# A PEER layer's look-ups: the factor of the gathered rows in PSUM, a quarter of the low parts on VectorE, and another order of choices

## The chip, the cores and the metric

The kernel runs on one core of a Trainium2 chip. The metric is the device time of one execution in microseconds (us). The engines are PE (TensorE), DVE (VectorE), ACT (ScalarE), POOL (GpSimd) and SP (SyncE, here only a queue that starts DMAs).

## The reference, cut to what matters

The program is two transformer blocks on 512 tokens of width 1024. Only the last layer of the second block changes, a mixture of 16384 tiny experts (128 x 128 keys), of which each token uses 8 x 16:

```
q = (xt @ w_q).reshape(T, H, 2, PEER_DKEY // 2)
s = jnp.einsum('thcd,hcnd->thcn', q, sub_keys).astype(jnp.float32)
top_s, top_i = lax.top_k(s, K)
cand = (top_s[:, :, 0, :, None] + top_s[:, :, 1, None, :]).reshape(T, H, K * K)
...
best_s, best_j = lax.top_k(cand, K)
expert = jnp.take_along_axis(cand_i, best_j, axis=-1)
g = jax.nn.softmax(best_s, axis=-1).astype(u.dtype)
...
act = jax.nn.gelu(jnp.einsum('cd,chkd->chk', xc, u_tab[ec]), approximate=False)
return jnp.einsum('chk,chkd->cd', gc * act, v_tab[ec])
```

## The kernel before, in words

The tokens lie in four groups of 128. For group 0 and half of group 1 (64 tokens) the rows of `u_tab` that were chosen are gathered from HBM by indirect DMAs, 128 rows of 4 KB to a fetch, and multiplied by the token (`gscr`, on DVE, which sums as it multiplies). For the remaining 320 tokens the product with all 16384 rows of `u` is computed densely, in 128 blocks (`expert_block`): a block loads 512 KB of `u` (`wraw`, by SP), ACT rounds it to a high part `whi`, POOL subtracts to get the low part `wlo`, and PE makes 24 matmuls of 320 columns from the parts. Three buffers hold `wraw`, three `whi` and `wlo`.

`route` makes queries, scores and the two stages of top-k (`choose`, on DVE), and writes out where each chosen expert stands as a dense table `Gd` (`gates`: one-hot tables `oh` by DVE, scaled by ACT, multiplied on PE into `pg`, copied by ACT to `stg`, written by SP). Beside it run the dense blocks, whose results go to HBM (`Ad`). `combine` then reads `v_tab` (`vraw`), `Gd` (`rgat`) and `Ad` (`ract`) and adds up the result in PSUM: 128 times 18 matmuls of 512 columns (`acc`). What blocks and fetches `route` did not get to is done there.

The order is set by code: `route` goes block by block, adds `UCOST` to a credit, and emits pieces of the routing work (`choose` and `gates` are generators whose `yield` gives a cost) while the credit is positive. After each block it issues up to `RATE` steps of `gathered`; a step is one fetch (on POOL's queue) and the product of the row fetched six steps before. `self.limit` holds the steps back until the indices are known. There are 332 steps (192 fetches of `u` rows, 128 of `v` rows, and two lags of 6). `combine` spreads what steps are left evenly over its units, one for each of the 128 additions and one for each block still to be made. Engines work in order, each through its own list.

Of the kernel before, what the change touches and what calls it, by code (L numbers as in the profile page):

```python
# [7 lines left out]
F32 = mybir.dt.float32  # L8
# [4 lines left out]
AF = mybir.ActivationFunctionType  # L13
# [24 lines left out]
LEAD = 2  # L38
FLEAD = 4
LAST = 3  # L40
GCOST = 0.4
UCOST = 1.7
AHEAD = 3
RATE = 1.5


class Stream:


    def __init__(self, nc, pool, chunks, raw_bufs, split_bufs):  # L50
        self.nc, self.pool, self.chunks = nc, pool, chunks
        self.raw_bufs, self.split_bufs = raw_bufs, split_bufs
        self.raw, self.parts = {}, {}
        self.nd = self.ns = self.ng = 0
        self.on_vector, self.all_vector = ("cw1",), False

    def _load(self):
        i = self.nd
# [6 lines left out]
    def _split(self):  # L65
        i = self.ns
        while self.nd <= i:
            self._load()
        w = self.chunks[i][2]
        raw = self.raw.pop(i)  # L70
        hi = self.pool.tile([P, 1024], F32R, name=f"whi{i}", tag="whi", bufs=self.split_bufs)
        lo = self.pool.tile([P, 1024], F32R, name=f"wlo{i}", tag="wlo", bufs=self.split_bufs)
        self.nc.scalar.activation(hi[:, :w], raw[:, :w], AF.Copy)  # L73
        if self.all_vector or self.chunks[i][0] in self.on_vector and i % 2:
            self.nc.vector.tensor_tensor(lo[:, :w], raw[:, :w], hi[:, :w].bitcast(F32), op=ALU.subtract)
        else:
            self.last_split = self.nc.gpsimd.tensor_tensor(lo[:, :w], raw[:, :w], hi[:, :w].bitcast(F32),  # L77
                                                           op=ALU.subtract)
        self.parts[i] = (hi, lo)
        self.ns += 1  # L80
# [18 lines left out]
class Kernel:  # L99
# [1141 lines left out]
    def gathered(self, ep):  # L1241
# [11 lines left out]
        def after():  # L1253
            return self.tc.issue_after(self.last_gate.ins) if self.last_gate else ExitStack()

        jobs = [(self.xidx, k, self.xx, self.xact) for k in range(NX)]
        jobs += [(self.gidx, k, self.xr, self.gact) for k in range(P)]
        rows = {}
        for k in range(self.nu + lag):
            if k < self.nu:  # L1260
                rows[k] = fetch(a["peer_ur_2"], *jobs[k][:2])
            if k >= lag:
                _, c, x, acc = jobs[k - lag]
                scr = ep.tile([P, D], BF16, name="gscr", tag="gscr", bufs=1)
                with after():
                    nc.vector.scalar_tensor_tensor(scr, rows.pop(k - lag), 1.0, x, op0=ALU.mult,  # L1266
                                                   op1=ALU.mult, accum_out=acc[:, c:c + 1])
            if k == self.nu + lag - 1:
                self.act(self.gact, self.gact, AF.Gelu)
                nc.vector.tensor_tensor(self.gw, self.gw, self.gact, op=ALU.mult)  # L1270
            yield
# [22 lines left out]
    def route(self, ep, rp, pp):  # L1294
        tc, nc, a = self.tc, self.nc, self.a
        sk = rp.tile([P, 16, P], F32, name="sk", tag="cand")
        nc.sync.dma_start(sk, a["peer_sk"])

        iota_s = rp.tile([P, P], F32, name="iota", tag="tables")
# [30 lines left out]
            return qt  # L1330

        def scores(b, q):
            pc = pp.tile([P, 4, P], F32, name="psc", tag="psc", bufs=4)
            for tb in range(4):
                nc.tensor.matmul(pc[:, tb, :], q[:, tb * P:(tb + 1) * P], sk[:, b, :], start=True, stop=True)
            for tb in range(4):
                topk(tv[:, tb, b], tix[:, tb, b], pc[:, tb, :], mr[:, :P])
# [133 lines left out]
        def gates(tb, p0=0, p1=4):  # L1471
# [6 lines left out]
            for part in range(p0, p1):  # L1478
                self.write(len(self.pieces) - P // PIECE)
                stg = self.cp.tile([P, P, 32], F32, name="stg", tag="xlo" if part % 2 else "xhi")  # L1480
                for k in range(8):
# [1 line left out]
                    if x + 4 * AHEAD < 32 * p1:  # L1483
                        oh[x + 4 * AHEAD] = onehots(t, x + 4 * AHEAD)
                    J, I = oh.pop(x)
                    pg = pp.tile([P, 4, P], F32, name="pg", tag="psc", bufs=4)
                    for c in range(4):
                        nc.tensor.matmul(pg[:, c, :], J[:, c], I[:, c], start=True, stop=True)  # L1488
                    nc.scalar.activation(stg[:, :, 4 * k:4 * k + 4], pg.rearrange("p c i -> p i c"), AF.Copy)
# [30 lines left out]
        def routing():  # L1520
            yield from choose(1, 4, 4)
            self.limit = NX
            yield from choose(0)
            self.limit = self.total
            yield from choose(2)
            yield from both(gates(2), choose(3), 3)
            yield from gates(3)
            yield from gates(1, NX // 32, 4)
            yield from activate()
            yield from gates(1, 0, NX // 32)  # L1530

        e, work, credit = 0, routing(), 0.0
        with tc.manual_schedule(engines={mybir.EngineType.PE}):
            for b in range(8, 16):
                qt = query(b)
                if b >= 16 - EARLY:
                    self.stored_block(e, ep)
                    e += 1
                scores(b, qt[:, 0])
                if b == 9:  # L1540
                    for _ in choose(1, 0, 4):
                        pass
                    self.limit = NX // 2
                self.fetch_steps(1.0)
            while work:
                self.stored_block(e, ep)
                credit += UCOST
# [21 lines left out]
    def combine(self, ep, e):  # L1569
        tc, nc, a = self.tc, self.nc, self.a  # L1570
        with tc.tile_pool(name="pv", bufs=1) as vp, tc.tile_pool(name="pvp", bufs=1, space=PSUM) as pp:
            self.ws.all_vector = True
            ng = vp.tile([P, D], F32, name="ng")
            nc.gpsimd.dma_start(ng, a["norm_final_2"].to_broadcast([P, D]))
            vh = self.cp.tile([P, 4, D], F32R, name="vh", tag="xhi")
# [210 lines left out]
```

## Time and profile before

| | |
|---|---|
| time, median of 3 runs (lowest to highest) | 2519.85 us (2518.43 to 2522.0) |
| profiled execution: time, span | 2520.2 us, 2518.5 us |
| busy share of the span | PE 93%, PE weight loads 78%, DVE 74%, ACT 46%, POOL 48% |
| HBM traffic over the span | 501 MB moved, mean 199 GB/s |

The span is the profiled part of the execution; 1.7 us of the time lie around it. The shares are means over stages with different limits, so what follows is read by stage. A PE instruction's recorded length overlaps the next one's, so a busy PE is not a PE at its peak; the distance between starts tells its pace.

### The profile page before, as it was taken

What the parts mean: (1) busy time and instruction counts of PE and PEld (TensorE: products, weight loads), DVE (VectorE), ACT (ScalarE), POOL (GpSimd) and SP (SyncE); (2) the same over time, 40 slices, a digit from 0 to 9 for tenths busy, and PEclk for the clock granted to TensorE, in tenths of its full rate; (3) what the DMA queues carried; (4) which work ended last, traced back from release to release, by engine and by line L of the source; (5) the groups of instructions that cost most, each with busy time, mean ns of one, the idle gap of its engine ahead of it and who ended that gap; (6) DMA issues with size and microseconds to landing.
All of it is one profiled execution on the core that took longest, in us unless ns stands there. A gap on an engine that the chain in (4) does not pass through costs nothing.

```text
span 2518.5 us, 33280 instructions
## 1 busy us (share of the span) xinstructions
PE 2344.5 (93%) x11872; PEld 1961.3 (78%) x11872; DVE 1871.1 (74%) x3095; ACT 1158.6 (46%) x2187; POOL 1219.7 (48%) x689
## 2 busy tenths in 40 slices
PE   7999999999999999999698777898999899999998
PEld 6766888887766668877597767788898788888887
DVE  7986777612475753457959999799887678998885
ACT  5665333322475664444223322365797343434343
POOL 5322444444623215533358878998766323433330
PEclk9999999999999999999898999999999999999999
DMA  4211323233313112222248878999988999999994
GB/s 135 68 51 51 99 94 101 88 96 113 117 44 126 34 34 89 95 93 75 73 162 260 290 258 276 309 321 325 346 319 310 366 330 380 379 380 377 379 378 136
DMA packets 205175, 501.05 MB, mean 199 GB/s; under 512 B 19424, under 2 KB 101504, under 8 KB 201808
## 3 DMA queue, kind: packets, MB, share of 16 engines
q1 hardware_dynamic: 138256, 306.81, 36.4%
q0 software_dynamic: 46448, 168.63, 18.4%
q10 hardware_dynamic: 20304, 23.48, 2.6%
q8 instruction: 93, 1.52, 0.3%
q14 instruction: 74, 0.61, 0.1%
HBM read 451.27 MB, written 47.58 MB: 198 GB/s over the span
## 4 chain that ended last, share of the span: by engine, by line
PE 62%; DVE 18%; issue 6%; POOL 5%; ACT 5%; DMA 3%; ACTq 0%; DVEq 0%; POOLq 0%; SPq 0%
PE acc L1643 21%; PE mm L141 11%; PE mm L139 11%; PE mm L140 11%; DVE gscr L1266 4%; POOL wlo L77 4%; DVE cv L380 2%; POOL grow L1249 1%; ACT oh L1468 1%; PE pg L1488 1%; DMA wraw<-in_peer_u 1%; PE av L1012 1%; PE tr L666 1%; ACT whi L73 1%; DMA rgat<-Gd 1%
## 5 line engine op out<-in xcount | busy, mean ns | idle before, releaser
L77 POOL TENSOR_TENSOR wlo<-wraw,whi 128x1024 fp32r<-128x1024 f32 (+1 forms) x311 | 755.7, 2432 | 770.5 <-ACT whi L73 719.2
L73 ACT ACTIVATE whi<-wraw 128x1024 fp32r<-128x1024 f32 (+1 forms) x319 | 334.4, 1049 | 654.8 <-PE mm L140 284.9
L141 PE MATMUL mm<-ushi,wlo 128*128 128x320 f32 x1024 | 334.2, 326 | 75.6 <-POOL wlo L77 75.2
L139 PE MATMUL mm<-xhi,whi 128*128 128x512 f32 x952 | 384.5, 404 | 4.7 <-DVE gb L408 2.1
L141 PE MATMUL mm<-xhi,wlo 128*128 128x512 f32 x952 | 377.3, 396 | 1.3 <-POOL wlo L77 1.2
L140 PE MATMUL mm<-xlo,whi 128*128 128x512 f32 x952 | 377.0, 396 | 0.0
L139 PE MATMUL mm<-ushi,whi 128*128 128x320 f32 x1024 | 332.1, 324 | 17.1 <-ACT act L122 10.0
L140 PE MATMUL mm<-uslo,whi 128*128 128x320 f32 x1024 | 328.0, 320 | 0.0
L1643 PE MATMUL acc<-vl,gahi 128*128 128x512 f32 x768 | 299.1, 390 | 0.0
L1643 PE MATMUL acc<-vh,galo 128*128 128x512 f32 x768 | 299.1, 389 | 0.0
L1643 PE MATMUL acc<-vh,gahi 128*128 128x512 f32 x768 | 299.1, 389 | 0.0
L1249 POOL DMA_INDIRECT grow<-in_peer_v,gidx x128 | 163.1, 1274 | 272.6 <-DVE gacc L1277 248.2
L141 PEld LDWEIGHTS mm<-ushi,wlo 128*128 128x128 f32 x1024 | 202.6, 198 | 89.3 <-POOL wlo L77 88.3
L1266 DVE SCALAR_TENSOR_TENSOR gscr<-grow,xr 128x1024 bf16<-128x1024 f32 x128 | 235.8, 1842 | 11.8 <-DMA grow<-in_peer_ur,gidx 10.2
L139 PEld LDWEIGHTS mm<-ushi,whi 128*128 128x128 f32 x1024 | 203.4, 199 | 19.9 <-ACT act L122 12.0
L139 PEld LDWEIGHTS mm<-xhi,whi 128*128 128x128 f32 x952 | 180.3, 189 | 46.9 <-issue 9.3
L140 PEld LDWEIGHTS mm<-xlo,whi 128*128 128x128 f32 x952 | 179.8, 189 | 40.4 <-issue 4.5
L141 PEld LDWEIGHTS mm<-xhi,wlo 128*128 128x128 f32 x952 | 180.0, 189 | 39.6 <-POOL wlo L77 1.9
L1249 POOL DMA_INDIRECT grow<-in_peer_ur,gidx x128 | 170.3, 1331 | 80.4 <-DVE gscr L1266 57.2
L140 PEld LDWEIGHTS mm<-uslo,whi 128*128 128x128 f32 x1024 | 202.6, 198 | 0.3
L196 ACT ACTIVATE gahi<-gg 128x384 fp32r<-128x384 f32 x128 | 67.3, 526 | 288.9 <-PE acc L1643 287.6
L1643 PEld LDWEIGHTS acc<-vh,galo 128*128 128x128 f32 x768 | 144.2, 188 | 30.0
(451 smaller groups left out, 4600.8 us busy)
## 6 DMA issues: line engine op xcount, KB each, us to landing
wraw<-in_peer_u SPq DMA_DIRECT2D x128, 512.0 KB, 4.8
vraw<-in_peer_v SPq DMA_DIRECT2D x128, 512.0 KB, 8.0
Gd<-stg SPq DMA_DIRECT2D x24, 1024.0 KB, 7.9
rgat<-Gd SPq DMA_DIRECT2D x32, 768.0 KB, 11.8
wraw<-in_w_up SPq DMA_DIRECT2D x44, 512.0 KB, 3.4
Ad<-act ACTq DMA_DIRECT2D x124, 160.0 KB, 4.8
ract<-Ad SPq DMA_DIRECT2D x124, 160.0 KB, 7.8
wraw<-in_w_in SPq DMA_DIRECT2D x20, 512.0 KB, 3.5
```

Of the source, the lines that this page charges most:

```text
L73: self.nc.scalar.activation(hi[:, :w], raw[:, :w], AF.Copy)
L77: self.last_split = self.nc.gpsimd.tensor_tensor(lo[:, :w], raw[:, :w], hi[:, :w].bitcast(F32), op=ALU.subtract)
L139: mm(ps, w[0], x[0], start=start, stop=False)
L140: mm(ps, w[0], x[1], start=False, stop=False)
L141: mm(ps, w[1], x[0], start=False, stop=stop)
L196: self.nc.scalar.activation(hi, src, AF.Copy)
L380: nc.vector.scalar_tensor_tensor(c, x, w, c, op0=ALU.mult, op1=ALU.add)
L666: nc.tensor.transpose(pt[:, qb - kb, :], W[:, c:c + P], self.ident)
L1012: nc.tensor.matmul(av[hs, kb * P:], Vb[i][:, kb, hs], PT[s][:, ks], start=False, stop=True, skip_group_check=True)
L1249: nc.gpsimd.indirect_dma_start(out=t, out_offset=None, in_=tab.rearrange("a b d -> (a b) d"), in_offset=bass.IndirectOffsetOnAxis(ap=idx[: ...
L1266: nc.vector.scalar_tensor_tensor(scr, rows.pop(k - lag), 1.0, x, op0=ALU.mult, op1=ALU.mult, accum_out=acc[:, c:c + 1])
L1643: mm(acc[tb][h], x[:, ts], v[:, i % 4, ds], start=False, stop=(i == P - 1 and x is lo), skip_group_check=True)
```

## The change

The row that the fetched rows are multiplied by is copied once to PSUM (`xps`, two banks, ACT) and read from there in `route`; in `combine` it is read from SBUF as before. `psc`, the PSUM buffers that scores and `pg` share, go from four to two. Every fourth low part of `u` (chunk number modulo 4 equal to 1) is made by DVE. The first half choice of group 1 is spread over four query steps; the order of choices and look-ups becomes: choice 1b, choice 2, look-ups 2 with choice 0 between, look-ups of the second half of group 1 with choice 3 between, look-ups 3, activation, look-ups of the first half of group 1. Three costs of the plan change.

```
-GCOST = 0.4
-UCOST = 1.7
+GCOST = 1.0
+UCOST = 2.4
...
-RATE = 1.5
+RATE = 1.4
...
-        self.on_vector, self.all_vector = ("cw1",), False
+        self.on_vector, self.all_vector = {"cw1": 2, "u": 4}, False
...
-        if self.all_vector or self.chunks[i][0] in self.on_vector and i % 2:
+        if self.all_vector or i % self.on_vector.get(self.chunks[i][0], 1) == 1:
...
+        def source(x):
+
+            if self.xps is None:
+                return
+            for h in range(2):
+                hs = slice(h * 512, (h + 1) * 512)
+                nc.scalar.activation(self.xps[:, hs], x[:, hs], AF.Copy)
+
...
+                if k - lag in (0, NX):
+                    source(x)
+                x = x if self.xps is None else self.xps
...
+        self.xps = pp.tile([P, D], F32, name="xps")
...
-            pc = pp.tile([P, 4, P], F32, name="psc", tag="psc", bufs=4)
+            pc = pp.tile([P, 4, P], F32, name="psc", tag="psc", bufs=2)
...
-                    pg = pp.tile([P, 4, P], F32, name="pg", tag="psc", bufs=4)
+                    pg = pp.tile([P, 4, P], F32, name="pg", tag="psc", bufs=2)
...
-            yield from choose(0)
+            yield from choose(2)
+            yield from both(gates(2), choose(0), 3)
             self.limit = self.total
-            yield from choose(2)
-            yield from both(gates(2), choose(3), 3)
+            yield from both(gates(1, NX // 32, 4), choose(3), 2)
             yield from gates(3)
-            yield from gates(1, NX // 32, 4)
...
-                if b == 9:
-                    for _ in choose(1, 0, 4):
-                        pass
-                    self.limit = NX // 2
+                if b == 8:
+                    early = choose(1, 0, 4)
+                for _ in range((1, 1, 1, 3, 0, 0, 0, 0)[b - 8]):
+                    next(early)
                 self.fetch_steps(1.0)
+            for _ in early:
+                pass
+            self.limit = NX // 2
...
             self.ws.all_vector = True
+            self.xps = None
```

On DVE, in the stretch of `route` where choices run beside dense blocks, the list before holds the products of fetched rows (`gscr`, with the token row `xx`) between pieces of a choice (`ixf`, `cand`, `bv`, `bix`, `mr`):

```order
1403 L1390 TENSOR_TENSOR cand<-tv 128x8x16
1404 L1266 SCALAR_TENSOR_TENSOR gscr,xact<-grow,xx 128x1024
1405 L1390 TENSOR_TENSOR cand<-tv 128x8x8
1406 L1266 SCALAR_TENSOR_TENSOR gscr,xact<-grow,xx 128x1024
1407 L1314 MAX bv<-cand 128x8 x2
1408 L1266 SCALAR_TENSOR_TENSOR gscr,xact<-grow,xx 128x1024
1409 L1315 MAX_INDEX bix<-bv,cand 128x8
1410 L1316 MATCH_REPLACE mr<-bv,cand 128x64
```

In the same stretch it now holds the products with `xps`, and a low part `wlo` on which PE waits:

```order
1457 L1277 SCALAR_TENSOR_TENSOR gscr,xact<-grow,xps 128x1024
1458 L1429 TENSOR_SCALAR mr<-pf 128x128
1459 L1385 TENSOR_TENSOR tmp<-tmp,tr 128x2048
1460 L75 TENSOR_TENSOR wlo_10960<-wraw_10905,whi_10959 128x1024
1461 L1431 SCALAR_TENSOR_TENSOR mask<-mr 128x128
1462 L1277 SCALAR_TENSOR_TENSOR gscr,xact<-grow,xps 128x1024
```

The operand `xx` became `xps`, and a low part stands in DVE's list behind the choice's work.

On POOL, in the same stretch, the list before has a low part for every block, with one or two fetches (`grow`) behind it:

```order
264 L77 TENSOR_TENSOR wlo_10486<-wraw_10445,whi_10485 128x1024
265 L1249 DMA grow<-in_peer_ur,xidx 128x1024 x2
266 L77 TENSOR_TENSOR wlo_10549<-wraw_10483,whi_10548 128x1024
267 L1249 DMA grow<-in_peer_ur,xidx 128x1024
268 L77 TENSOR_TENSOR wlo_10588<-wraw_10546,whi_10587 128x1024
```

Now a block in four is missing from it, and its fetches stand with those of the block before:

```order
257 L77 TENSOR_TENSOR wlo_10521<-wraw_10474,whi_10520 128x1024
258 L1249 DMA grow<-in_peer_ur,xidx 128x1024
259 L77 TENSOR_TENSOR wlo_10563<-wraw_10518,whi_10562 128x1024
260 L1249 DMA grow<-in_peer_ur,xidx 128x1024 x3
261 L77 TENSOR_TENSOR wlo_10643<-wraw_10602,whi_10642 128x1024
```

The low part between the first and the second of the three fetches moved to DVE.

On DVE in `combine`, each addition has a split (`vl`), the weights (`gg`, `galo`) and the products of fetched `v` rows (`gacc`); before, one for most additions:

```order
2046 L1623 TENSOR_TENSOR vl<-vraw,vh 128x1024
2047 L1277 SCALAR_TENSOR_TENSOR gacc<-grow,gw,gacc 128x1024
2048 L197 TENSOR_TENSOR galo<-gg,gahi 128x384
2049 L1628 TENSOR_TENSOR gg<-rgat,ract 128x320
2050 L1623 TENSOR_TENSOR vl<-vraw,vh 128x1024
2051 L1277 SCALAR_TENSOR_TENSOR gacc<-grow,gw,gacc 128x1024
```

Now one and two in turn:

```order
2060 L1638 TENSOR_TENSOR vl<-vraw,vh 128x1024
2061 L1288 SCALAR_TENSOR_TENSOR gacc<-grow,gw,gacc 128x1024 x2
2062 L197 TENSOR_TENSOR galo<-gg,gahi 128x384
2063 L1638 TENSOR_TENSOR vl<-vraw,vh 128x1024
2064 L1643 TENSOR_TENSOR gg<-rgat,ract 128x320
2065 L1288 SCALAR_TENSOR_TENSOR gacc<-grow,gw,gacc 128x1024
```

More of the fetches fall behind `route`, so an addition carries more of them.

## Rows read from the trace of the kernel before

**Rows 1.** Busy time by stretch: us, then busy us of each engine with instruction counts.

```profile
core 0: us, PE busy (x) PEld busy (x) DVE busy (x) ACT busy (x) POOL busy (x), PEclk, DMA share, GB/s
1163.00:1330.00 167.00, 147.69 (x803) 127.75 (x802) 130.76 (x626) 47.82 (x86) 70.51 (x34) 0.95 0.35 114
1330.00:1640.00 310.00, 240.77 (x1449) 228.89 (x1448) 290.10 (x491) 94.97 (x141) 271.45 (x149) 0.93 0.85 280
1640.00:1790.00 150.00, 135.05 (x937) 131.44 (x936) 140.22 (x137) 94.19 (x215) 133.51 (x74) 0.98 0.94 329
1790.00:1950.00 160.00, 150.36 (x1061) 145.63 (x1059) 131.39 (x141) 136.97 (x363) 100.10 (x58) 0.96 0.87 322
...
2050.00:2470.00 420.00, 420.00 (x1855) 347.88 (x1854) 374.24 (x436) 169.77 (x309) 153.90 (x121) 1.00 1.02 369
```

**Rows 2.** Groups by line, 1330 to 1640: busy us, mean ns, idle before and releaser.

```profile
L141 PE MATMUL mm<-ushi,wlo 128*128 128x320 f32 x481 | 161.1, 335 | 67.4 <-POOL wlo L77 67.4
...
L77 POOL TENSOR_TENSOR wlo<-wraw,whi 128x1024 fp32r<-128x1024 f32 x60 | 147.6, 2461 | 1.1
L1266 DVE SCALAR_TENSOR_TENSOR gscr<-grow,xx 128x1024 bf16<-128x1024 f32 x62 | 122.6, 1977 | 1.4 <-DMA grow<-in_peer_ur,xidx 1.4
...
L1249 POOL DMA_INDIRECT grow<-in_peer_ur,xidx x57 | 82.1, 1440 | 31.7 <-issue 5.6 <-DVE gscr L1266 5.3 <-DVE wsm L1408 4.4
L73 ACT ACTIVATE whi<-wraw 128x1024 fp32r<-128x1024 f32 x60 | 63.5, 1058 | 213.1 <-DMA wraw<-in_peer_u 159.0 <-PE mm L140 44.2 <-PE mm L141 9.8
L1266 DVE SCALAR_TENSOR_TENSOR gscr<-grow,xr 128x1024 bf16<-128x1024 f32 x26 | 61.1, 2349 | 8.0 <-DMA grow<-in_peer_ur,gidx 7.4
```

**Rows 3.** Timeline of DVE and POOL near 1377 us: start us, length us, instruction.

```profile
1376.76 3.94 DVE L1266 SCALAR_TENSOR_TENSOR gscr<-grow,xx 128x1024 bf16<-128x1024 f32 x1
1377.26 2.35 POOL L77 TENSOR_TENSOR wlo<-wraw,whi 128x1024 fp32r<-128x1024 f32 x1
...
1380.84 1.21 DVE L1266 SCALAR_TENSOR_TENSOR gscr<-grow,xx 128x1024 bf16<-128x1024 f32 x1
```

**Rows 4.** Views of line L1463 and tile gscr: ns min/median/max, first and last start.

```profile
L1463 DVE TENSOR_TENSOR oh<-tables,ijwT x96: 1206/1215/1226, 1627.3 to 1941.5; 128x1024 f32<-128x1024 f32 x96
...
L1266 DVE SCALAR_TENSOR_TENSOR gscr<-grow,xr x128: 1206/1226/3996, 1555.1 to 2033.3; 128x1024 bf16<-128x1024 f32 x128
```

**Rows 5.** Tiles psc and ident, and a wait from 1163 to 1330 us.

```profile
L1335 PE MATMUL psc<-sk,pq x128: 271/276/378, 1172.6 to 1318.8; 128*128 128x128 f32 x128
...
L1649 PE MATMUL acc<-ident,xT x48: 274/276/377, 1950.0 to 1955.4; 128*128 128x128 f32 x48
...
PE tr L1454 <- DVE tmp L1373: 16.9, 1, 16.9
```

**Rows 6.** PE's timeline: matmuls 2 and 24 of a block, three look-up steps.

```profile
1560.05 0.31 PE L139 MATMUL mm<-ushi,whi 128*128 128x320 f32 x1
...
1563.28 0.31 PE L140 MATMUL mm<-uslo,whi 128*128 128x320 f32 x1
...
1855.92 2.84 PE L1488 MATMUL pg<-oh 128*128 128x128 f32 x24
```

**Rows 7.** An ACT group from 1790 to 1950 us.

```profile
L1489 ACT ACTIVATE stg<-pg 128x512 f32<-128x512 f32 x64 | 36.3, 581 | 0.1
```

**Rows 8.** DVE's groups from 2050 to 2470 us.

```profile
L1277 DVE SCALAR_TENSOR_TENSOR gacc<-grow,gw,gacc 128x1024 f32<-128x1024 f32 x127 | 162.6, 1280 | 0.9
L1623 DVE TENSOR_TENSOR vl<-vraw,vh 128x1024 fp32r<-128x1024 f32 x103 | 125.5, 1219 | 0.0
L197 DVE TENSOR_TENSOR galo<-gg,gahi 128x384 fp32r<-128x384 f32 x103 | 57.5, 558 | 42.9 <-ACT gahi L196 42.9
```

**Rows 9.** Two stretches of 20 us, columns as in rows 1.

```profile
1790.00:1810.00 20.00, 16.38 (x118) 16.00 (x117) 18.89 (x18) 13.92 (x35) 16.79 (x10) 0.94 1.02 404
...
2310.00:2330.00 20.00, 20.00 (x90) 16.58 (x89) 18.13 (x23) 8.22 (x15) 8.56 (x7) 1.00 1.04 386
```

**Rows 10.** The page's DMA issues: count, KB each, median us to landing.

```profile
vraw<-in_peer_v SPq DMA_DIRECT2D x128, 512.0 KB, 8.0
...
rgat<-Gd SPq DMA_DIRECT2D x32, 768.0 KB, 11.8
...
ract<-Ad SPq DMA_DIRECT2D x124, 160.0 KB, 7.8
```

## The prediction

> **What bounds the kernel now.** I read the busy times by stretch first. The part behind 2050 us is the additions: PE is busy for all of it and starts 1855 matmuls in 420 us, 226 ns each, so an addition (18 matmuls) takes 4.08 us; DVE is busy for 374 of the 420 us and the DMA engines' share is 1.02 at 369 GB/s [rows 1]. Nothing there waits, but little is left on DVE and DMA. Between the last score (1318.8 us) and the first matmul of `combine` (1950.0 us) [rows 5] lie 631 us in which `route` runs. By its costs (193.2 units, 1.7 a block) it makes 114 blocks there behind the 8 of the query steps, 122 in all. PE needs 3.23 us for 22 steps of a block, so 3.52 us for 24, and 2.84/3 = 0.95 us for a look-up step [rows 6]: 114 blocks and 96 steps are 401 + 91 = 492 us. The other 139 us are waits, and that is what the change can take.
>
> What sets the pace there changes on the way. From 1330 to 1640 us 60 blocks take 310 us, 5.17 each; DVE is busy for 290 us, POOL for 271 [rows 1]. PE waits 67 us for POOL's low parts; ACT waits 159 us for `wraw`, whose three buffers come free when a low part is done: a ring through POOL [rows 2]. DVE's 88 products take 122.6 + 61.1 us, 2.09 each [rows 2], though the shortest takes 1.21 [rows 4]. The timeline says why: one that began at 1376.76 ended at 1380.70, 1.09 us behind the end of POOL's low part, which ran from 1377.26 to 1379.61; the next, with no low part beside it at first, took 1.21 [rows 3]. A product that reads two SBUF operands stands still while POOL subtracts. From 1640 to 1790 DVE is still the busiest (140 of 150 us). From 1790 to 1950, with 64 look-up steps [rows 7] and 24 blocks, PE needs 145 of 160 us and ACT is busy for 137 [rows 1].
>
> **The change, part by part.** *The factor in PSUM.* No row shows this product with a PSUM operand. The nearest is `oh`, the same 1024 elements with one PSUM operand, made beside POOL's low parts: 1206/1215/1226 ns in 96 cases, never held [rows 4]. I take 1.22 us; the other end is 2.09, no change. The copies into PSUM are four ACT instructions of the size of `stg`, 0.58 us each [rows 7]: 2.3 us, beside an ACT with 213 us idle in 310 [rows 2]. The second pair must wait for the last product with the first row; the fetches pause there anyway, so I take nothing. With no cover it is some 4 us.
>
> *Low parts on DVE.* 26 of the 105 blocks behind the queries. POOL's work falls from 2.46 + 1.5 x 1.44 = 4.62 us a block to 0.75 x 2.46 + 1.4 x 1.44 = 3.86 [rows 2], so the ring no longer rules. A low part on DVE still has two SBUF operands: between 1.22 us and the 2.09 of the products that were held. I take 2.0, since POOL still subtracts 3 blocks in 4. It stands in DVE's list behind choice work, and PE's next block waits for it; two blocks of splits are made ahead, some 9 us. On who is held, the Trainium skill (SBUF — State Buffer, Who interferes with whom) says that the pair's port goes whole to the instruction that starts first. The row shows a DVE product that started 0.5 us earlier and was held all the same [rows 3]. By the rule half of the 26 would cost 1.22, 10 us of DVE work less in all; I go by the row.
>
> *The plan.* The costs now sum to 250.8 units, 2.4 a block: 105 blocks, 113 in all. 9 blocks move behind `route`: 9 x 3.52 = +32 us there. A unit of choice was about 1 us of DVE: 290 - 184 us for 60 x 1.7 = 102 units [rows 1, 2]. Walking through the generators gives four stretches; in each I take the engine with most work.
> Blocks 8 to 35, choices alone: DVE 67 us of choice, 39 products x 1.22, 7 low parts x 2.0 = 129; PE 99.
> Blocks 36 to 64, choice 0 with 32 look-up steps: PE 29 x 3.52 + 30 = 132; DVE 35 + 35 x 1.22 + 25 x 1.22 + 14 = 122.
> Blocks 65 to 87, choice 3 with 16 steps: DVE 36 + 19 + 39 + 12 = 106; PE 96.
> Blocks 88 to 112, 48 steps: PE 88 + 46 = 134; ACT has fewer steps than the 64 that kept it busy for 137 us [rows 1, 7].
> Sum 501 us. Before, the same measure gives 310/290 = 1.07, 150/140 = 1.07 and 160/145 = 1.10 of the busiest engine. I take 1.09, as PE rules half of it: 546 us against 631, **-85 us**. Ends: 1.03 gives 516, DVE without its gain 637 (below).
>
> *The query steps.* PE waited 16.9 us once for the first choice [rows 5]; spread over four steps it is done when PE comes to it. With two `psc` buffers instead of four PE may wait for DVE's top-k at the last scores, up to two of some 7 us as the wait moves. I take **-12 us**, ends 0 and -17. `pg` with two buffers: ACT's `stg` of 0.58 us [rows 7] is shorter than PE's 0.95 us for a step, and PE's list has at most three steps in a row; the factor 1.09 holds it.
>
> *The additions.* When `route` ends, 176 of the 332 steps were done before (7 with the queries, 1.5 a block); now 131 (1.4 a block, less 15 for 11 blocks held by the limit). `combine` has 128 additions and now 12 new blocks (113 and the two unwritten pieces round up to 116), so 201 steps over 134 units are 1.5 a unit against 156/126 = 1.24. An addition with a stored block moved 524 + 197 + 164 KB of `vraw`, a quarter of `rgat`, and `ract` [rows 10], and 1.24 fetches of 524: 1535 KB in 4.08 us, 376 GB/s, as measured (369). Now it is 1671 KB, 410 GB/s. The highest stretches show 404 (in `route`) and 386 (here) [rows 9]. At the middle, 395, an addition takes 4.23 us: 116 x 0.15 = **+17 us**. Ends: at 410 nothing, at 369 4.53 us, +52. DVE's work rises from 374/103 = 3.63 us an addition by 0.26 x 1.28 to 3.97 [rows 1, 8]: under 4.08, if it no longer waits the 42.9/103 = 0.4 us for ACT, which the second product fills.
>
> Sum: -85 - 12 + 32 + 17 = -48. The profiled execution took 2520.2 us (span 2518.5), 0.35 over the median, so **2472 us**.
>
> **The rivals.**
> *PSUM does not free the product* (chance 0.05). What I call holding would be something else, and a product stays at 2.09 us. The four stretches become 163, 144, 134 and 143 us, 584 x 1.09 = 637: +6 - 12 + 32 + 17 = +43, 2563 us, slower. It decides from a product of about 1.7 us on. Against it: 96 `oh` rows never held.
> *DVE's low parts are late* (0.10). A full choice is some 36 us of DVE work by its costs, in lumps; if each of 26 makes PE wait 1.5 us more than now, 39 us go: 2511; from 1.9 us each on nothing is left. For it: DVE was 94% busy from 1330 to 1640; against it, the load falls.
> *The additions saturate the DMA engines at 369 GB/s* (0.12): the share was 1.02 already [rows 1]. +52 instead of +17: 2507 us.
> *The DMA engines take it all* (0.15): the rows show no ceiling, only demand met. Additions stay at 4.08 us: 2455 us. The Trainium skill (DMA: Bandwidth & Descriptors, Bandwidth, Measured) gives 425 GB/s to one core alone, over the 410 that are asked, so by it this rival holds; no run here shows it.
> *Route waits less than before* (0.08): factor 1.03, with the ring gone: 30 us less, 2442 us.
>
> **How the numbers follow.** The forecast has 0.50. 2444 to 2510 leaves out the slower rival, half of late low parts and half of the last rival, and the tails of the others, under 2 in 10. A measurement of this kernel tells 0.2% (5 us) from no change. Faster by more: 0.86 (the forecast, saturation, the two faster ones, part of late low parts); within: 0.05; slower: 0.09 (the first rival, low parts over 2 us late).
>
> **What the profile after would show.** Right: `gscr` near 1.22 us in `route` without a tail to 4 us; `wlo` on DVE near 2 us; `combine` starting near 1853 us; PE's wait for low parts well under 67 us; additions at 4.1 to 4.4 us with a DMA share over 1.02. Wrong: `gscr` still near 2 us; PE's waits for DVE's low parts adding to over 40 us; or additions over 4.5 us, with PE idle behind `vl` or `galo`.

## The result and the profile after

The changed kernel takes **2419.45 us** (median of 4 runs, 2415.80 to 2423.28); the kernel before took 2520.91 us beside it. The ratio is 0.9599, interval 0.9581 to 0.9617: 101 us faster, where 48 were forecast, and below the range of 2444 to 2510. The profiled execution took 2417.63 us, its span 2415.9, so 102.6 us of span are to be accounted for. Three places give them, and they are the three of the prediction's sum.

The tiles `psc`, `acc` with `ident`, and `gscr` (ns min/median/max, first and last start) answer to [rows 4] and [rows 5]:

```profile
L1347 PE MATMUL psc<-sk,pq x128: 270/275/377, 1170.0 to 1299.2; 128*128 128x128 f32 x128
...
L1664 PE MATMUL acc<-ident,xT x48: 275/275/377, 1805.5 to 1810.8; 128*128 128x128 f32 x48
...
L1277 DVE SCALAR_TENSOR_TENSOR gscr<-grow,xps x125: 1196/1209/1223, 1315.3 to 1801.5; 128x1024 bf16<-128x1024 f32 x125
```

| | before | after | moved | forecast |
|---|---|---|---|---|
| last score | 1318.8 | 1299.2 | -19.6 | -12 |
| last score to first matmul of `combine` | 631.2 | 506.3 | -124.9 | -85 |
| from there to the end of the span | 568.5 | 610.4 | +41.9 | +49 |

The product with `xps` is what was forecast, 1.21 us and never held: 125 of them lie between 1196 and 1223 ns, where before one of the same kind could take 3996 [rows 4]. So this mechanism stands, and the miss is in the sizes. Most of it, 40 of 55 us of span, lies in the middle row. Busy time by stretch there, at the four ends of the walk through the generators (block 35, 64, 87 and the last), then for the whole of it and for the additions; columns as in [rows 1]:

```profile
core 0: us, PE busy (x) PEld busy (x) DVE busy (x) ACT busy (x) POOL busy (x), PEclk, DMA share, GB/s
1299.20:1417.00 117.80, 105.36 (x690) 103.74 (x689) 114.74 (x321) 44.35 (x63) 90.28 (x58) 0.96 0.89 320
1417.00:1561.00 144.00, 133.54 (x934) 132.25 (x934) 120.18 (x206) 97.29 (x225) 78.25 (x49) 0.96 0.82 293
1561.00:1666.00 105.00, 99.21 (x689) 98.42 (x688) 75.76 (x91) 62.14 (x127) 75.61 (x49) 0.97 0.91 330
1666.00:1805.50 139.50, 135.61 (x1002) 134.23 (x1000) 108.51 (x135) 118.40 (x294) 80.84 (x56) 0.99 0.94 352
1299.20:1805.50 506.30, 473.73 (x3308) 468.64 (x3306) 419.20 (x752) 322.18 (x707) 324.99 (x210) 0.97 0.89 323
1900.00:2380.00 480.00, 472.96 (x2130) 392.87 (x2129) 434.35 (x539) 190.74 (x340) 231.45 (x163) 0.99 1.04 381
```

And the same stretch before, of which [rows 1] had only parts:

```profile
1318.80:1950.00 631.20, 537.38 (x3520) 517.16 (x3518) 572.56 (x812) 330.02 (x723) 511.64 (x282) 0.95 0.88 301
```

PE went from 85% to 94% busy, DVE from 91% to 83%, POOL from 81% to 64%. PE is now the busiest engine in three of the four stretches; in the first it is still DVE, but with 114.7 us where the forecast had given it 129.

Groups by line, 1300 to 1805 us, answer to [rows 2]:

```profile
L141 PE MATMUL mm<-ushi,wlo 128*128 128x320 f32 x840 | 264.4, 315 | 18.1 <-DVE wlo L75 18.1
...
L77 POOL TENSOR_TENSOR wlo<-wraw,whi 128x1024 fp32r<-128x1024 f32 x78 | 188.3, 2415 | 111.8 <-ACT whi L73 110.8
...
L1277 DVE SCALAR_TENSOR_TENSOR gscr<-grow,xps 128x1024 bf16<-128x1024 f32 x125 | 151.3, 1210 | 6.3 <-ACT xps L1262 3.5 <-DMA grow<-in_peer_ur,xidx 2.2
...
L73 ACT ACTIVATE whi<-wraw 128x1024 fp32r<-128x1024 f32 x105 | 110.8, 1055 | 141.6 <-PE mm L140 59.3 <-DMA wraw<-in_peer_u 52.8 <-issue 8.7
...
L1249 POOL DMA_INDIRECT grow<-in_peer_ur,gidx x67 | 68.9, 1029 | 43.9 <-DVE gscr L1277 30.4 <-issue 4.9 <-PE pg L1500 2.8
L1249 POOL DMA_INDIRECT grow<-in_peer_ur,xidx x63 | 67.0, 1063 | 25.4 <-DVE gscr L1277 13.0 <-issue 5.9 <-PE mm L140 1.3
...
L75 DVE TENSOR_TENSOR wlo<-wraw,whi 128x1024 fp32r<-128x1024 f32 x27 | 39.5, 1462 | 18.4 <-ACT whi L73 18.1
```

PE's wait for a low part, 67.4 us in 310 before and 75.2 in all 631, is 18.1 us in 505, and it is for DVE's low parts, not POOL's. ACT's wait for `wraw` fell from 159 to 53 us: the ring through POOL is gone, and POOL itself waits 111 us for ACT. A low part on DVE took 1.46 us, not 2.0. One thing was not in the prediction at all: a fetch costs POOL 1.03 to 1.06 us where it cost 1.44.

In the page's DMA issues, both loads of `combine` land later than in [rows 10]: 12.2 us instead of 8.0, 11.3 instead of 7.8.

```profile
vraw<-in_peer_v SPq DMA_DIRECT2D x128, 512.0 KB, 12.2
...
ract<-Ad SPq DMA_DIRECT2D x116, 160.0 KB, 11.3
```

### The profile page after: what moved, and what is told of

Its sections match the earlier page's. It is cut to its first block, busy times and chain, and to the rows that moved or that the text cites. A ratio compares the mean times of both kernels' runs of the same rounds, so it can differ in the third digit from the quotient of the medians.

```text
span 2415.9 us, 33346 instructions
## 1 busy us (share of the span) xinstructions
PE 2313.0 (96%) x11872; PEld 1941.4 (80%) x11872; DVE 1774.6 (73%) x3131; ACT 1167.0 (48%) x2191; POOL 1105.0 (46%) x653
## 4 chain that ended last, share of the span: by engine, by line
PE 55%; DVE 19%; DMA 14%; issue 5%; ACT 4%; POOL 1%; SPq 0%; DVEq 0%; ACTq 0%; POOLq 0%
PE mm L139 12%; PE mm L140 12%; PE mm L141 12%; PE acc L1658 8%; DMA vraw<-in_peer_v 7%; DMA ract<-Ad 4%; PE pg L1500 3%; DVE cv L380 2%; DVE gscr L1277 2%; DMA wraw<-in_peer_u 1%; POOL wlo L77 1%; DVE gacc L1288 1%; PE av L1012 1%; DVE wlo L75 1%; PE tr L666 1%
## 5 line engine op out<-in xcount | busy, mean ns | idle before, releaser
L77 POOL TENSOR_TENSOR wlo<-wraw,whi 128x1024 fp32r<-128x1024 f32 (+1 forms) x275 | 662.8, 2412 | 835.3 <-ACT whi L73 770.4
L141 PE MATMUL mm<-ushi,wlo 128*128 128x320 f32 x1024 | 321.7, 314 | 18.1 <-DVE wlo L75 18.1
L140 PE MATMUL mm<-uslo,whi 128*128 128x320 f32 x1024 | 320.7, 313 | 0.0
L1249 POOL DMA_INDIRECT grow<-in_peer_v,gidx x128 | 180.6, 1411 | 183.4 <-DVE gacc L1288 156.9
L1249 POOL DMA_INDIRECT grow<-in_peer_ur,gidx x128 | 151.7, 1186 | 153.4 <-DVE gscr L1277 134.1
L141 PEld LDWEIGHTS mm<-ushi,wlo 128*128 128x128 f32 x1024 | 196.4, 192 | 20.2 <-DVE wlo L75 20.2
L1637 ACT ACTIVATE vh<-vraw 128x1024 fp32r<-128x1024 f32 x128 | 135.1, 1056 | 154.5 <-DMA vraw<-in_peer_v 145.7
L139 PEld LDWEIGHTS mm<-ushi,whi 128*128 128x128 f32 x1024 | 196.9, 192 | 11.2 <-ACT act L122 10.5
L1638 DVE TENSOR_TENSOR vl<-vraw,vh 128x1024 fp32r<-128x1024 f32 x128 | 156.2, 1220 | 43.8 <-ACT vh L1637 43.2
L1658 PEld LDWEIGHTS acc<-vl,gahi 128*128 128x128 f32 x768 | 144.8, 189 | 35.6 <-DVE vl L1638 5.9
## 6 DMA issues: line engine op xcount, KB each, us to landing
vraw<-in_peer_v SPq DMA_DIRECT2D x128, 512.0 KB, 12.2
ract<-Ad SPq DMA_DIRECT2D x116, 160.0 KB, 11.3
```

The lines of the kernel that those rows point to most:

```text
L139: mm(ps, w[0], x[0], start=start, stop=False)
L140: mm(ps, w[0], x[1], start=False, stop=False)
L141: mm(ps, w[1], x[0], start=False, stop=stop)
L1249: nc.gpsimd.indirect_dma_start(out=t, out_offset=None, in_=tab.rearrange("a b d -> (a b) d"), in_offset=bass.IndirectOffsetOnAxis(ap=idx[: ...
L1637: nc.scalar.activation(vh[:, i % 4, :], r, AF.Copy)
L1638: nc.vector.tensor_tensor(vl[:, i % 4, :], r, vh[:, i % 4, :].bitcast(F32), op=ALU.subtract)
```

## The experiments

The kernel before ran beside all of them, with medians of 2519.26 to 2521.82 us. The letters of the theories are those of the expectations: A is the prediction's account, in which the stretch of `route` shrinks since products are no longer held and the plan alone gives nothing; by B the ring through POOL sets the pace; C gives the plan a gain of its own.

| kernel | time, us | ratio [95% interval] | last score to `combine`, us | behind, us |
|---|---|---|---|---|
| before + factor in PSUM | 2464.44 | 0.9793 [0.9764, 0.9822] | 577.1 | 565.1 |
| before + low parts on DVE | 2490.12 | 0.9884 [0.9858, 0.9910] | 602.8 | 567.5 |
| before + both | 2457.19 | 0.9742 [0.9717, 0.9766] | 574.1 | 565.5 |
| plan alone | 2463.88 | 0.9776 [0.9748, 0.9805] | 542.3 | 613.8 |
| after, factor in SBUF | 2452.60 | 0.9729 [0.9707, 0.9751] | 534.7 | 612.6 |
| after, no low parts on DVE | 2412.18 | 0.9565 [0.9543, 0.9588] | 498.3 | 610.8 |
| after, every second on DVE | 2415.49 | 0.9584 [0.9563, 0.9604] | 503.7 | 608.3 |
| before, `RATE` 1.1 | 2502.34 | 0.9922 [0.9895, 0.9949] | 580.9 | 601.9 |
| after, `RATE` 2.3 | 2441.93 | 0.9686 [0.9663, 0.9710] | 536.7 | 601.2 |
| before, new `GCOST`, `UCOST` | 2486.82 | 0.9868 [0.9845, 0.9891] | 565.2 | 601.0 |
| after, old `GCOST`, `UCOST` | 2463.75 | 0.9773 [0.9747, 0.9798] | 551.8 | 611.8 |
| before, first choice spread | 2496.61 | 0.9913 [0.9884, 0.9943] | 622.8 | 569.1 |
| after, first choice at once | 2433.80 | 0.9657 [0.9640, 0.9675] | 500.0 | 612.9 |
| after, old order of choices | 2415.58 | 0.9590 [0.9569, 0.9612] | 510.9 | 601.4 |
| after, no low parts, `RATE` 1.2 | 2413.83 | 0.9572 [0.9555, 0.9589] | 497.5 | 620.6 |

The last two columns are of the profiled execution of each kernel; that of the last row took some 15 us more than its median.

**The factor alone.** The kernel before, with `xps`, its copies and the two `psc` buffers that make room for it:

```
...
+                if k - lag in (0, NX):
+                    source(x)
+                x = x if self.xps is None else self.xps
...
+        self.xps = pp.tile([P, D], F32, name="xps")
...
-            pc = pp.tile([P, 4, P], F32, name="psc", tag="psc", bufs=4)
+            pc = pp.tile([P, 4, P], F32, name="psc", tag="psc", bufs=2)
...
-                    pg = pp.tile([P, 4, P], F32, name="pg", tag="psc", bufs=4)
+                    pg = pp.tile([P, 4, P], F32, name="pg", tag="psc", bufs=2)
...
```

> The kernel before with one part of the change: the products of route read the token row from PSUM (and psc has two buffers, since the banks are needed); low parts and plan as before. Theory A (operand: the products' standing still beside POOL's low parts cost the time): a product at 1.21 us instead of 1.95 takes DVE off the limit; 64 blocks of choices then need 233 us of DVE, 267 of POOL, so route ends some 60 us earlier and the time is 2460 us (2440 to 2480). Theory B (low parts: the ring through POOL, low part done, buffer free, next load, sets the pace): POOL's work of 4.6 us a block stays, 5 to 15 us gained, 2505 to 2515. Theory C (plan: the order of choices and look-ups): 0 to 15 us gained.

2464.44 us, 55 us faster as A had it, and nearly all of it in `route` (631 to 577 us). Its groups there:

```profile
L141 PE MATMUL mm<-ushi,wlo 128*128 128x320 f32 x912 | 287.0, 315 | 12.7 <-POOL wlo L77 12.6
...
L1277 DVE SCALAR_TENSOR_TENSOR gscr<-grow,xps 128x1024 bf16<-128x1024 f32 x170 | 205.9, 1211 | 33.0 <-DMA grow<-in_peer_ur,gidx 31.0 <-DMA grow<-in_peer_ur,xidx 1.1
L1249 POOL DMA_INDIRECT grow<-in_peer_ur,gidx x111 | 105.8, 953 | 59.3 <-DVE gscr L1277 38.0 <-issue 13.8 <-DVE wsm L1419 1.3
```

The same three of before:

```profile
L141 PE MATMUL mm<-ushi,wlo 128*128 128x320 f32 x912 | 298.4, 327 | 75.2 <-POOL wlo L77 75.2
...
L1266 DVE SCALAR_TENSOR_TENSOR gscr<-grow,xr 128x1024 bf16<-128x1024 f32 x108 | 211.3, 1957 | 11.6 <-DMA grow<-in_peer_ur,gidx 10.2
L1249 POOL DMA_INDIRECT grow<-in_peer_ur,gidx x110 | 149.2, 1357 | 37.6 <-DVE gscr L1266 16.7 <-issue 15.7 <-DVE oh L1463 0.5
```

Two gains show. DVE's product falls from 1.96 to 1.21 us; and POOL's fetch falls from 1.36 to 0.95, with POOL's low parts nearly as long as before (2404 against 2469 ns). POOL's busy time falls from 512 to 433 us with the same work. PE's wait for low parts all but ends, 75 to 13 us; its waits for ACT's `act` rise from 8 to 30 us and those for `stg` come to 16, so not all of it is won. The product that was held held POOL too: by the timeline of the kernel before, the 59 fetches in `route` that began with no product running on DVE took 0.93 to 1.01 us; the 109 that began while one ran had a median of 1.76. With the factor in PSUM none of the first 64 takes longer than 1.05 us. The fetches of that kind (ns min/median/max), before and with the factor:

```profile
L1249 POOL DMA_INDIRECT grow<-in_peer_ur,xidx x64: 936/1348/1957, 1258.2 to 1532.2; - x64
...
L1249 POOL DMA_INDIRECT grow<-in_peer_ur,xidx x64: 933/950/1051, 1257.9 to 1489.0; - x64
```

**The low parts alone, and beside the factor.** The edit in the kernel before, without and with the edit above:

```
-        self.on_vector, self.all_vector = ("cw1",), False
+        self.on_vector, self.all_vector = {"cw1": 2, "u": 4}, False
...
-        if self.all_vector or self.chunks[i][0] in self.on_vector and i % 2:
+        if self.all_vector or i % self.on_vector.get(self.chunks[i][0], 1) == 1:
```

> The kernel before with every fourth low part of u on DVE, nothing else. Theory A: DVE gets 0.5 us a block more while its products are still held: same or up to 20 us slower, 2520 to 2540. Theory B: POOL's 4.6 us a block become 3.9, a gain of 30 to 45 us, 2475 to 2490. Theory C: no gain, within 10 us of before.

> The kernel before with the token row in PSUM (two psc buffers) and every fourth low part on DVE; plan as before. If operand (-53 us alone) and low parts (-29 alone) take away the same thing, the mutual holding of DVE and POOL, they do not add: 2455 to 2470. If each takes a limit of its own (DVE's products, the ring through POOL), they add: 2430 to 2445.

Alone, 2490.12 us: 29 us faster, at the edge of what B had; A, by which it would be slower, is wrong here. Beside the factor it adds 7 us, with intervals that overlap. The two relieve the same thing, so they don't add. In the first of them, DVE's groups in `route`:

```profile
L1266 DVE SCALAR_TENSOR_TENSOR gscr<-grow,xr 128x1024 bf16<-128x1024 f32 x108 | 185.4, 1716 | 11.4 <-DMA grow<-in_peer_ur,gidx 10.5
...
L1266 DVE SCALAR_TENSOR_TENSOR gscr<-grow,xx 128x1024 bf16<-128x1024 f32 x64 | 110.4, 1725 | 1.0 <-DMA grow<-in_peer_ur,xidx 1.0
...
L75 DVE TENSOR_TENSOR wlo<-wraw,whi 128x1024 fp32r<-128x1024 f32 x29 | 39.4, 1359 | 3.1 <-ACT whi L73 3.1
```

DVE took over 39.4 us of low parts and its products took 295.8 us instead of 336.3 (211.3 and 125.0): the work that it took over came back, since POOL now subtracts 85 times instead of 114. A held product has no price of its own; it costs what the other engine's work makes of it. The rival of late low parts shows in this kernel too, as PE waits for DVE's:

```profile
PE mm L141 <- DVE wlo L75: 40.8, 10, 8.6
```

**The low parts in the full change.** After, with none and with half of them on DVE:

```
-        self.on_vector, self.all_vector = {"cw1": 2, "u": 4}, False
+        self.on_vector, self.all_vector = {"cw1": 2}, False
```

> The kernel after with all low parts of u on POOL: operand in PSUM and plan. Adding singles gives 2520 - 53 - 56 = 2411 with low parts worth nothing more; if the low parts still relieve the ring, 2425 to 2450.

> The kernel after with every second low part of u on DVE in place of every fourth (the suspected cost of these low parts doubled). With none on DVE the time was 2412. If a low part on DVE costs PE waits (18 us in the trace after) and POOL no longer is a limit: 2425 to 2445. If they are free: 2415 to 2423. If they still relieve POOL: under 2412.

2412.18 us with none, 2415.49 with half, 2419.45 with a quarter; the intervals overlap, and the times don't follow the share. So no gain of the quarter shows here. With none, PE waits 7.5 us for POOL's low parts, and with half 19.3 for DVE's:

```profile
L141 PE MATMUL mm<-ushi,wlo 128*128 128x320 f32 x840 | 262.1, 312 | 7.5 <-POOL wlo L77 7.5
...
L141 PE MATMUL mm<-ushi,wlo 128*128 128x320 f32 x843 | 263.4, 313 | 19.3 <-DVE wlo L75 19.3
```

Once products don't hold it, POOL is quick enough for all, and a low part in DVE's list only comes late at times.

**The plan alone, and the change without the factor.** After, with `xps` taken away (the token row from SBUF), and for the first also the low parts back on POOL and four `psc` buffers:

```
-        self.xps = pp.tile([P, D], F32, name="xps")
+        self.xps = None
```

> The kernel after with both other parts taken back: the token row read from SBUF, psc with four buffers, all low parts of u on POOL; order of choices and look-ups, the three costs and the spread first choice as after. Theory A: DVE has 2.4 units of choice and 1.4 held products a block, 5.3 us or more; nothing gained in route, and 32 us of blocks moved behind it: 2520 to 2550. Theory B: 2510 to 2530. Theory C: most of the gain, 2440 to 2470.

> The kernel after with the token row read from SBUF again, as before; everything else as after (two psc buffers, low parts, plan). Theory A: products back at 1.8 to 2.1 us, most of the gain lost, 2490 to 2540. Theory B and theory C: little lost, 2420 to 2440.

The plan alone gives 56 us, 2463.88, and A fell in this: by it the plan had no gain of its own. C has the size. With the low parts as well it is 2452.60 us, where the prediction's first rival, in which products stay slow, came to 2563; its products took 1.70 and 1.74 us, and its time lies in none of the expected ranges. The plan alone, `route` and its product of the first row:

```profile
1304.30:1846.60 542.30, 482.56 (x3308) 474.04 (x3307) 492.15 (x723) 318.12 (x705) 439.20 (x234) 0.95 0.87 301
...
L1277 DVE SCALAR_TENSOR_TENSOR gscr<-grow,xx 128x1024 bf16<-128x1024 f32 x64 | 131.6, 2057 | 0.3
```

Products are held as ever, 2.06 us. But the stretch has nine blocks fewer and 127 products instead of 172: the products take 73 us less of DVE (263 for 336), whose busy time falls by 80. Plan (56) and factor (55) then add in full: 2520 - 111 = 2409, and with both and no low parts on DVE 2412 was measured.

**Parts of the plan: where fetches go.** `RATE` alone, first in the kernel before (132 steps in `route` instead of 176), then in after (174 instead of 131):

```
-RATE = 1.5
+RATE = 1.1
```

```
-RATE = 1.4
+RATE = 2.3
```

> The kernel before with one number changed, RATE 1.1 in place of 1.5: 132 of the 332 steps are done in route, as in the kernel after, in place of 176. If what the plan gains (-56 us alone) is the 44 held products (2 us of DVE, 1.4 us of POOL each) that it moves behind route, where POOL makes no low parts, this gives most of it: 2465 to 2485. If the plan gains by the order of choices and look-ups, 2505 to 2525.

> The kernel after with one number changed, RATE 2.3 in place of 1.4: 174 steps in route, about as many as before. If the fetches' place carries the plan's gain also with the operand in PSUM, route gets 43 x 1.29 us of DVE and 43 x 1.06 us of POOL back, and the additions fall to their 4.08 us: 2430 to 2450. If place does not matter once products are not held, within 8 us of after, 2412 to 2428.

In the kernel before, 44 steps moved behind `route` take 50 us out of it and put 33 behind: 17 us faster, between the two expected ranges. In after, 43 steps moved into `route` put 30 us into it and give back 9 behind: 22 us slower. A step is dearer in `route` both times, even with products of 1.21 us.

**Parts of the plan: how much `route` does.**

```
-GCOST = 0.4
-UCOST = 1.7
+GCOST = 1.0
+UCOST = 2.4
```

> The kernel before with the two costs alone (GCOST 1.0, UCOST 2.4): 113 blocks in route instead of 122, 164 steps instead of 176; operand in SBUF, all low parts on POOL, order, RATE and first choice as before. If the denser routing work per block is the rest of what the plan gains (-56, of which the first choice some 15 and the fetches' place some 17): 2490 to 2503. If nine blocks are only moved behind and DVE, with 2.4 units of choice and 1.5 held products a block, sets the pace: 2515 to 2535.

> The kernel after with the two costs as before (GCOST 0.4, UCOST 1.7): 122 blocks in route, 126 steps; all else as after. If the costs carry some 20 us: 2435 to 2450. If they only move blocks: 2412 to 2427.

In before, 32 us faster; undone in after, 44 slower: more than was expected both times. Busy time in `route`, the new costs in the kernel before:

```profile
1318.50:1883.70 565.20, 488.45 (x3304) 474.94 (x3302) 545.11 (x788) 318.53 (x705) 497.95 (x262) 0.95 0.90 314
```

Nine blocks and 12 steps less take 66 us out of `route` and put 32.5 behind it, where a block has PE's own 3.52 us and its low part comes from DVE: the forecast's +32. PE had no wait there from 1980 to 2440 us, so the 12 steps that went with the blocks cost it none. In `route` they had cost 7.3 us each with their steps, not the 5.17 of [rows 1]: PE's busy time falls by 49 us, POOL's by only 14, and PE's wait for low parts from 75 to 46:

```profile
PE mm L141 <- POOL wlo L77: 45.7, 35, 4.0
```

**Parts of the plan: the first choice, and the order.** The first choice spread over query steps in the kernel before; made at once in after (the same edit backwards); and after with the order of choices and look-ups of before:

```
-                if b == 9:
-                    for _ in choose(1, 0, 4):
-                        pass
-                    self.limit = NX // 2
+                if b == 8:
+                    early = choose(1, 0, 4)
+                for _ in range((1, 1, 1, 3, 0, 0, 0, 0)[b - 8]):
+                    next(early)
...
+            for _ in early:
+                pass
+            self.limit = NX // 2
```

```
-            yield from choose(2)
-            yield from both(gates(2), choose(0), 3)
+            yield from choose(0)
...
-            yield from both(gates(1, NX // 32, 4), choose(3), 2)
+            yield from choose(2)
+            yield from both(gates(2), choose(3), 3)
...
+            yield from gates(1, NX // 32, 4)
```

> The kernel before with the first half choice of group 1 spread over four query steps as after (fetches let go behind the query steps), nothing else. If the wait of 16.9 us is all of it: 2502 to 2508. If it is worth less while route's DVE is the limit: 2508 to 2518.

> The kernel after with the first half choice of group 1 made at once in the second query step with a score, as before, and its fetches let go from there. The trace before has one wait of 16.9 us of PE there. If that wait is the whole of it, 12 to 20 us are lost: 2431 to 2440; if the seven fetches that then run in the query steps give something back, 2422 to 2430.

> The kernel after with the order of choices and look-ups as before (choice 0 in second place, choice 3 beside look-ups 2, then look-ups 3 and 1 in a row); costs, operand and low parts as after. Since choice 0 is ready sooner, the fetches are not held and 146 steps fall in route instead of 131. If the order itself (look-ups spread, so that ACT and PE do not pile up at the end) carries the rest of the plan's gain: 2435 to 2455. If the costs and the spread first choice carry it: 2415 to 2430, of which up to 8 for the 15 steps.

Spreading gives 23 us in before (the last score comes 13.6 us sooner, `route` is 8 shorter), more than was expected, and 14 in after. PE's waits from 1163 to 1330 us, in after with the choice made at once, have the wait of [rows 5] back:

```profile
PE tr L1466 <- DVE tmp L1385: 16.9, 1, 16.9
```

In after itself the longest of that kind is 4.5 us for `pq`. The order of choices and look-ups, as tried, gives nothing: 2415.58 us against 2419.45, intervals nearly the same. With the old order 15 more products fall in `route` (140 with `xps` instead of 125), so what the order alone does isn't shown.

**A faster one?** After without low parts on DVE and with `RATE` 1.2:

```
-RATE = 1.4
+RATE = 1.2
...
-        self.on_vector, self.all_vector = {"cw1": 2, "u": 4}, False
+        self.on_vector, self.all_vector = {"cw1": 2}, False
```

> The kernel after with no low part of u on DVE and RATE 1.2 in place of 1.4: 121 steps in route instead of 131, to see on which side the limit of the additions lies and as a candidate for the fastest version. If the additions still have room on the DMA engines (385 GB/s in the trace after): 2404 to 2411. If they are at their limit, ten fetches more behind cost 10 x 524 KB at 385 GB/s, 14 us, less some 5 us won in route: 2417 to 2425.

2413.83 us, no better than with 1.4, and between the two expected ranges. The fastest kernel here is after without low parts on DVE, 2412.18 us; the intervals of the two ratios touch (0.9543 to 0.9588 against 0.9581 to 0.9617), so that it beats the changed kernel is likely and not shown.

## Why the prediction was right, and where it was wrong

*The factor in PSUM: right.* 1.22 us forecast, 1.21 measured, no tail. Its rival (product still 2.09) is out. What it left out is POOL's share of the gain: fetches at 1.44 us in the sum, 0.95 to 1.06 in the runs with `xps`.

*The stretch of `route`: the step that failed.* The term of -85 us took the busiest engine's load in each of four stretches, 501 us, times 1.09: 546. It measured 506, 125 us less than before. PE's loads were near, 99 + 132 + 96 + 134 = 461 us against 474 busy. DVE's were too high where they set the pace: 129 and 106 us in the first and third stretch against 114.7 and 75.8 busy (in the second 122 against 120.2). With the measured ones DVE rules the first stretch alone, and the sum is 114.7 + 132 + 96 + 134 = 477; times 1.09 that is 520. So some 26 of the 40 us lie in DVE's loads. The other 14 lie in the factor, which came out at 506/477 = 1.06: `route` waited less than the forecast let it, which is half the way to the rival with 1.03. Why it did stays open.

In the first stretch most of DVE's 14 us is a count. The forecast charged 39 products; 31 ran. No fetch ran in the query steps (the first begins at 1298.6 us), so the first six steps of `route` have a fetch and no product. DVE's two large groups from 1299.2 to 1417 us:

```profile
L1277 DVE SCALAR_TENSOR_TENSOR gscr<-grow,xps 128x1024 bf16<-128x1024 f32 x31 | 37.4, 1206 | 2.3 <-DMA grow<-in_peer_ur,xidx 2.2
L75 DVE TENSOR_TENSOR wlo<-wraw,whi 128x1024 fp32r<-128x1024 f32 x7 | 12.8, 1825 | 0.0
```

They leave 64.5 us for the 67 units of choice, so a unit at 1 us was near there, and a low part took 1.83 us. Over the first three stretches 113.5 us are left for 138 units, 0.82 each, and 16 of them in the third stretch, where 36 were charged. Part of that is place: DVE works ahead of the walk. That it is holding undone is not shown: what is left of DVE's busy time in all of `route` beside products, tables and low parts is 122.7 us before, 133.2 with the factor alone and 109.2 after. A low part took 1.46 us on average where 2.0 were charged. That is some 9 us for the 20 of the first three stretches.

*The rival of 2563 us.* It held the plan's gain to be the factor's, and charged DVE 584 us in `route`, where after with the factor in SBUF has 481.5 busy: its products took 1.72 us, not 2.09, with 78 low parts on POOL instead of 105. The runs show two gains of about equal size, each there without the other (55 and 56 us), and the plan's comes from three places that overlap: costs 32, first choice 23, fetches 17, together 72 against 56.

*The query steps: nearly right.* -19.6 us against -12. The wait of 16.9 us went whole, and the fear for two `psc` buffers was for nothing: with them alone the last score stayed at 1318.4. In the ten traces with the first choice spread the last score lies between 1299.2 and 1309.1 us, and the changed kernel's is the earliest of them; so some of the 19.6 is the luck of this execution.

*Nine blocks moved behind: right*, 32 forecast, 32.5 measured in the kernel before with the new costs, where 12 steps moved with them and cost PE no wait.

*The additions: price right, total less.* From 1900 to 2380 us PE starts 2130 matmuls, of which 192 belong to 8 blocks; with 3.52 us for a block an addition took 4.20 us, where 4.23 was forecast. Over all, 41.9 less 32 leaves +10 of the +17; with `RATE` 2.3, where PE never waited, 601.2 us lie behind, 9 less. The DMA rate, taken as 395 GB/s, was 381 over the stretch, and PE waited only 4.0 us for `vh` and 3.0 for `vl` from 1840 to 2400 us: the loads' 12 us are mostly covered by what is loaded ahead.

*The low parts on DVE*: nothing in the full change, where the prediction needed them to break POOL's ring. The factor alone had cut PE's wait for low parts to 13 us. The rival of late low parts is seen in part: PE's wait for them is 18.1 us, under the 40 that would have counted. They were dearer in the forecast than on the chip, because most of them met no subtraction on POOL. By the timeline of the 27 in `route`, the 7 that took 1.43 to 2.97 us began while a low part ran on POOL. The other 20 took 1.21 to 1.23 us; one of them had a POOL low part beside it, which began 0.23 us later and took 3.25 us itself. By the Trainium skill (SBUF — State Buffer, Who interferes with whom) the instruction that starts first gets the port; these eight agree. In the kernel before, of 42 products in `route` that a POOL low part joined within their first 1.21 us, 27 were not held and 15 were, as in [rows 3]; so the rule decides most cases and not all. One of the seven:

```profile
1336.30 2.37 POOL L77 TENSOR_TENSOR wlo<-wraw,whi 128x1024 fp32r<-128x1024 f32 x1 [1.49 <-ACT whi L73]
...
1337.20 2.56 DVE L75 TENSOR_TENSOR wlo<-wraw,whi 128x1024 fp32r<-128x1024 f32 x1
```

*The signs.* The product without a tail, the wait for low parts and the additions (4.20 us, DMA share 1.04) came as the prediction had them; `wlo` at 1.46 us and the start of `combine` at 1805.5 instead of 1853 us did not.

Still open: the parts of the plan were each tried in one direction on each kernel, so that how they share their overlap is not settled, and why a step costs more in `route` than behind it, with products of 1.21 to 1.22 us on both sides in after, is not either.

## What to carry to other kernels

A price that is read from a stretch in which two engines hold each other is no price for the stretch without it: list what an instruction takes when nothing holds it (the shortest row) beside the mean, and ask for each instruction of both engines what would still run beside it after the edit. Here that gives the product 1.21 us, a fetch 0.95 instead of 1.44 and most of DVE's low parts 1.22 instead of 2.0. And count a stretch's instructions from where its pipeline starts: a lag of six fetches took six products out of the first stretch. Two edits that relieve the same wait don't add; two that take work out of a stretch and waits out of it may, so run each alone before the whole. And a block of work is worth moving when its price where it is (7.3 us here, with its steps and the waits) is over that where it goes (3.6).

## What the runs showed of the hardware

Holding goes both ways. With the product's factor in PSUM, POOL's indirect fetch took 0.95 us where it had taken 1.36 to 1.43, in a kernel that changed nothing on POOL. That DVE's product isn't held agrees with the Trainium skill (SBUF — State Buffer, Who interferes with whom), by which a DVE instruction with at most one SBUF input, outside the modes that take both ports, does not contend with GpSimd; 125 rows of 1196 to 1223 ns show it here. What a fetch waits for, the timelines show. In after the fetches in `route` that began with no product from SBUF and no low part running on DVE took at most 1.02 us; most of the 20 that began beside one, nearly always a low part, took 1.67 to 1.96. One of them:

```profile
1422.64 1.22 DVE L75 TENSOR_TENSOR wlo<-wraw,whi 128x1024 fp32r<-128x1024 f32 x1
...
1422.99 1.68 POOL L1249 DMA_INDIRECT grow<-in_peer_ur,xidx  x1 [4.83 <-DVE gscr L1277]
```

Without low parts on DVE a fetch in `route` took 0.95 to 0.96 us on average, so they are what makes it 1.03 to 1.06 in the changed kernel. And the prediction's "stands still while POOL subtracts" is too wide: in the kernel before, the product of [rows 3] that began at 1380.84 us took 1.21, and the POOL low part that began beside it, at 1381.55, took 2.73 where that of [rows 3] took 2.35.

The DMA engines moved no more than 381 to 384 GB/s over a long stretch, in three kernels with different plans, at a share of 1.04 or 1.05: the additions of after, of before with `RATE` 1.1 and of after with the old costs. PE waited 7, 19 and 23 us for `vh` and `vl` there. Where they moved less (352 to 369 GB/s) PE was busy for all of the stretch, and in the kernel before also from 2100 to 2400 us, at 377 to 380. So the waits begin close to 380; that this is the engines' own limit is not shown. The two, in order, of before with `RATE` 1.1:

```profile
2000.00:2450.00 450.00, 430.95 (x1842) 348.27 (x1841) 401.01 (x495) 171.90 (x307) 224.72 (x156) 0.98 1.05 384
```

and of after with `RATE` 2.3:

```profile
1930.00:2390.00 460.00, 460.00 (x2098) 385.55 (x2098) 391.34 (x458) 185.06 (x334) 156.00 (x125) 1.00 0.98 352
```
